# A decoder layer with product-key experts: the branch for the rest of the lists moves from the middle of the second expert product to its end

## The chip, the cores and the metric

The kernel runs on one NeuronCore of a Trainium2 chip. The metric is the device time of one launch in microseconds. Engines go by the names of the profile: PE is TensorE (PEld its weight loads), DVE is VectorE, ACT is ScalarE, POOL is GpSimd, SP is SyncE, which issues DMAs. Each engine runs its instructions in order and waits on semaphores.

## The reference

One layer for 256 tokens of width 2048: an input projection, two kinds of attention, an output projection, and then three residual steps, each with a layer norm. The change lies in the second step, the expert layer. Each token has 8 heads; each head picks 16 of 16,384 experts by two lists of 128 sub-keys.

```python
def peer_ffn(x, wq, sub_keys, u, v):
    ...
    eidx = jnp.take_along_axis(cidx, sel, axis=-1)
    gates = jax.nn.softmax(top, axis=-1)
    ...
        ub = u[eb]
        vbk = v[eb]
        act = jax.nn.gelu(jnp.einsum('thed,td->the', ub, xb).astype(jnp.float32))
        w = (gb * act).astype(xb.dtype)
        return jnp.einsum('the,thed->td', w, vbk)
...
x = layer_norm(alpha * x + ffn_out, ln_g[i, 1], ln_b[i, 1])
gate = jax.nn.sigmoid(jnp.einsum('bsd,de->bse', x, ple_gate[i]))
emb = jnp.einsum('bsk,kd->bsd', p[i], ple_proj[i])
x = layer_norm(alpha * x + gate * emb, ln_g[i, 2], ln_b[i, 2])
```

## The kernel before, in words

The expert layer treats the tokens in two ways. For 168 of them (`NDT`) all experts are computed densely; for the other 88 (`NSP`) only the chosen rows are fetched.

*Dense, u.* For each of 128 blocks of 128 experts (`u_block`, line 1130), 1 MB of `peer_u` is loaded by SyncE into one of five buffers `wf`, and 16 matmuls give the activations of 168 tokens (`ps_u`, line 212). While they run, the gates of the dense tokens are made into a table by one-hot products (`gate_work`: `ps_G`, lines 970 and 971) and multiplied onto the activations (line 987). This is done in two parts, blocks 0 to 67 and 68 to 127. Then `list_work` counts which experts any token uses and makes a list of them, for each part; the activations themselves go to memory (`s_w`).

*Dense, v.* Only listed experts are used. A block of v takes 128 of a list: GpSimd issues two gathers by index, `wc` (the activations, 86 KB) and `vf` (the rows of v, 1 MB, line 1199), and TensorE does 16 matmuls into six banks of PSUM (`ps_v`, line 1228). The plan has 46 blocks for the first list and 40 for the second (`CAPS`). A list can be longer than its plan; the overhang is counted (`total`), read into a register (line 1271), and a branch on it (`tc.If`) runs the remaining 42 blocks, or none. With these inputs it runs none. Four blocks are fetched ahead (`LEAD`), in five buffers. The last three blocks (`STAG`) are held back and done bank by bank behind the loop, so that a finished bank can be added to the residual (`v_out`), transposed (`res2`) and normed while the next one runs.

*Sparse.* The 88 tokens stand in three groups (`GROUPS`); 88 gathers of 1 MB of u rows and 88 of v rows (`gb`, line 897, four buffers) are issued by GpSimd too. VectorE multiplies and adds each (lines 865, 875), which frees the buffer. They are spread over u and v by a pace: behind every block the pace is added to `due`, and each whole number issues one gather (`gathers`). `GU` is the pace in blocks 5 to 67 of u, `GUG` in the next 38, `GUL` in the last 22, `GVG` and `GV` in v. What is left at block 32 of the second list is issued at once. The sums of groups 1 and 2 go to their place by 64 small matmuls (`third_sums`, line 929), the ones of group 0 by `natural_out`.

*Order.* Instructions wrapped in `keep` stay in the order of the program on their engine; the others are placed by a scheduler that simulates the kernel. It doesn't move instructions across the branch. On the path round the body of the branch GpSimd waits on all its eight DMA semaphores, since the body would issue DMAs on them.

*Behind the expert layer.* The gate product loads `ple_gate` into the same five buffers (`sg2.load`), splits it (lines 121 and 122) and multiplies.

Of the kernel before, what the change touches and what calls it, by code (L numbers as in the profile page):

```python
# [23 lines left out]
ND = D // P  # L24
# [32 lines left out]


GQ = 1.8
GU, GUG, GUL = 0.77, 0.80, 0.5  # L60
GV, GVG = 0.63, 0.76
GSCALE = 2.0 ** 15
GB = 3
# [4 lines left out]
STAG, LEAD, NWC = 3, 4, 8  # L68
# [92 lines left out]
def build(tc, a, out):  # L161
    nc = tc.nc
    pools = Pools(tc)
# [5 lines left out]
    def pbank(pool, name, tag="bank", bufs=4):  # L169
        return pool.tile([P, 512], F32, name=name, tag=tag, bufs=bufs)  # L170
# [653 lines left out]
    def gathers(n):  # L824

        nonlocal due
        due += n
        while due >= 1:
            due -= 1
            run(sparse, 1)  # L830
# [78 lines left out]
    def natural_parts():  # L909

        for c in range(NCH):
            parts01.append(sg2.split(ys[0], c * 512))

    def natural_out(c):

        ps = pbank(pa, "ps_yn")
        for n, part in enumerate(parts01[c]):
            keep(nc.tensor.matmul(ps[:NNAT], sel[0], part, start=n == 0, stop=n == 1))
        s = slice(c * 512, (c + 1) * 512)
        keep(nc.vector.tensor_tensor(x2[0][:NNAT, s], x2[0][:NNAT, s], ps[:NNAT], op=ALU.add))  # L920
        for j in range(2):
            keep(nc.vector.bn_stats(st2[0][:NNAT, 2 * c + j, :],
                                    x2[0][:NNAT, c * 512 + j * 256:c * 512 + (j + 1) * 256]))

    def third_sums(ps, d0, d1):

        for d in range(d0, d1):
            for i in (1, 2):
                keep(nc.tensor.matmul(ps[:, d * 32:(d + 1) * 32], ys[i][:, d * P:(d + 1) * P],
                                      sel[i], start=i == 1, stop=i == 2))  # L930

    def third_out(ps):
        n = NSP - NNAT
        dst = XF[:, :, NNAT:NSP]
        keep(nc.vector.scalar_tensor_tensor(
            dst, dst, ALPHA, ps.rearrange("p (j t) -> p j t", j=ND)[:, :, :n],
            op0=ALU.mult, op1=ALU.add))
# [184 lines left out]
    def run(work, n):  # L1122

        for _ in range(n):
            if next(work, "end") == "end":
                return True
        return False
# [51 lines left out]
    a2p = pools.open("a2p", "left", bufs=1)  # L1179
    ohp = pools.open("ohp", "left", bufs=1)  # L1180
# [10 lines left out]
    rest = [(i, b) for i, (_, n) in enumerate(PARTS) for b in range(CAPS[i], n)]  # L1191

    def v_fetch(i, b, vpool, wpool, tags):

        vf = vpool.tile([P, D], F32, name="vf", tag=tags[0], bufs=WF if vpool is sup else 2)
        wc = wpool.tile([P, NDT], F32, name="wc", tag=tags[1], bufs=NWC if vpool is sup else 2)
        for dst, src, idx in ((wc, a[f"s_w{i}"].rearrange("p a t -> (p a) t"), idxW[i]),
                              (vf, a["v_rows"], idxV[i])):
            keep(nc.gpsimd.indirect_dma_start(  # L1199
                out=dst, out_offset=None, in_=src,  # L1200
                in_offset=bass.IndirectOffsetOnAxis(ap=idx[:, b:b + 1], axis=0)))
        return vf, wc
# [24 lines left out]
    def v_mm(d, vf, wc, last):  # L1227
        return nc.tensor.matmul(psv[d // 3][:, d % 3 * NDT:(d % 3 + 1) * NDT],  # L1228
                                vf[:, d * P:(d + 1) * P], wc, start=False,
                                stop=last and (d % 3 == 2 or d == ND - 1))  # L1230
# [8 lines left out]
    def v_out(b):  # L1239

        n = min(3, ND - 3 * b)
        dst = XF[:, 3 * b:3 * b + n, NSP:]
        keep(nc.vector.scalar_tensor_tensor(
            dst, dst, ALPHA, psv[b][:, :n * NDT].rearrange("p (j t) -> p j t", j=n),
            op0=ALU.mult, op1=ALU.add))

    def v_blocks(n, wpool, between=lambda: None):

        for _ in range(n):
            while order and len(fetched) <= LEAD and (not order[0][0] or len(idxV) > 1):  # L1250
                fetched.append(v_fetch(*order.pop(0), sup, wpool, ("wf", "wc")))
            block = fetched.pop(0)
            for d in range(ND):
                v_mm(d, *block, False)
                if d % 8 == 7:
                    between()
# [10 lines left out]
    for b in range(CAPS[0]):  # L1267
        if b == CAPS[0] - LEAD:
            while not done:
                done = run(work, 1)  # L1270
            more = nc.values_load(total[0:1, 0:1], min_val=0, max_val=NIA * NKEY)
        v_blocks(1, wcp, half)
        gathers(GVG if b < 28 else GV)

    fbp = pools.open("fbp", "right", bufs=1)
    with tc.If(more > 0, preferred_fallthrough_block=False):
        for i, b in rest:
            block = v_fetch(i, b, fbp, fbp, ("vf", "wc_"))
            for d in range(ND):
                v_mm(d, *block, False)  # L1280
    pools.close("fbp", "ohp", "a2p")
    wcq = pools.open("wcq", "left", bufs=1)
    for _ in range(LEAD + 1):
        v_blocks(1, wcq)
# [11 lines left out]
    def res2(t, d0, nd):  # L1296

        ps = pbank(pp, "ps_y2")
        for j in range(nd):
            keep(nc.tensor.transpose(ps[:, j * P:(j + 1) * P], XF[:, d0 + j, t * P:(t + 1) * P],  # L1300
                                     ident))
        r = slice(0 if t else NNAT, P)
        for c in range(nd // 2):
            nc.vector.bn_stats(st2[t][r, d0 // 2 + c, :], ps[r, c * 256:(c + 1) * 256])
        nc.scalar.copy(x2[t][r, d0 * P:(d0 + nd) * P], ps[r, :nd * P])
# [11 lines left out]
    def rows2(c):  # L1317
        for i, src in enumerate(("ln_g", "ln_b")):
            keep(nc.sync.dma_start(
                gb2[c][:, i], a[src][1:2, c * 512:(c + 1) * 512].to_broadcast([P, 512])))  # L1320
# [5 lines left out]
    def res1(d0, nd):  # L1326

        ps = pbank(pa, "ps_y1")
        for j in range(nd):
            keep(nc.tensor.transpose(ps[:, j * P:(j + 1) * P], XF[:, d0 + j, :P], ident))  # L1330
        nc.scalar.mul(x2[0][:NNAT, d0 * P:(d0 + nd) * P], ps[:NNAT, :nd * P], ALPHA)
# [8 lines left out]
    N1 = CAPS[1]  # L1340
    for b in range(LEAD + 1, N1 - STAG):
        v_blocks(1, wcq)
        gathers(GV)
        if b in range(6, 14, 2):
            res1(2 * b - 12, 4)
        if b == N1 - 20:
            natural_parts()
        if b in range(N1 - 18, N1 - 14):
            natural_out(b - N1 + 18)
        if b == N1 - STAG - 5:  # L1350
            while not run(sparse, 1):
                pass
    held = list(fetched)
    assert len(held) == STAG and not order
    gw = [sg2.load(a["ple_gate"][0, i]) for i in range(2)]
    parts0 = [sg2.split(gw[0], c * 512) for c in range(4)]

    for bank in range(6):
        if bank == 1:
            ps3 = pbank(pa, "ps_y3")  # L1360
            third_sums(ps3, 0, ND)
            third_out(ps3)
        elif bank == 2:
            res2(1, 0, 2)
            res2(0, 0, 2)
        elif bank == 3:
            res2(1, 2, 4)
            res2(0, 2, 4)
            rows2(0)
            parts0 += [sg2.split(gw[1], c * 512) for c in range(4)]  # L1370
        elif bank == 4:
            res2(1, 6, 2)
            res2(0, 6, 2)
            rows2(1)
        elif bank == 5:
            res2(1, 8, 4)
            res2(0, 8, 4)
        for d in range(3 * bank, min(3 * bank + 3, ND)):
            for i, block in enumerate(held):
                keep(v_mm(d, *block, i == STAG - 1))  # L1380
        v_out(bank)
# [346 lines left out]
```

## Time and profile before

| | |
|---|---|
| three runs | 1738.1, 1739.07, 1742.0 us (median 1739.07) |
| the profiled execution | 1734.96 us, its span 1733.2 us |
| mean granted TensorE clock | 0.989 |
| busy share | TensorE 98%, VectorE 64%, GpSimd 35%, ScalarE 32% |
| DMA | 555.49 MB, mean 321 GB/s |
| u, dense product | from 559 to 1161 us of the span |
| v, dense product | from 1163 to 1623 us of the span |
| branch | at about 1400 us |

Times in the rows are microseconds from the start of the span. A block of v is 32 records of `ps_v`, two for each matmul. Idle time stands in square brackets with what ended it. A stretch shows how long each engine was busy in it, the granted clock as a share of full speed (1.00 or 0.50 at any moment) and the share of time in which the 16 DMA engines were busy.

### The profile page before, as it was taken

How to read it: one execution, taken by the hardware profiler on the slowest of the kernel's cores; microseconds unless marked ns; L12 is line 12 of the kernel's file. 1: busy time of each engine (PE TensorE's matmuls, PEld its weight loads, DVE VectorE, ACT ScalarE, POOL GpSimd, SP SyncE). 2: the span in 40 equal slices, each digit the busy share in tenths (PEclk: the TensorE clock that was granted, in tenths of full speed). 3: DMA queues.
4: the chain of work that ended last, by engine and by line, in shares of the span. 5: the costliest groups of instructions: out<-in, count | busy, mean ns of one | idle time of the engine just before them, and what ended most of it. 6: DMA issues, size and time to landing. Idle time of an engine off the chain costs nothing.

```text
span 1733.2 us, 29306 instructions
## 1 busy us (share of the span) xinstructions
PE 1696.1 (98%) x11288; PEld 1574.4 (91%) x11288; DVE 1100.7 (64%) x2299; ACT 553.9 (32%) x1392; POOL 607.2 (35%) x625
## 2 busy tenths in 40 slices
PE   9999999999999999999999999999999989997998
PEld 7888888877889999999999999999999989997786
DVE  5565588662589779744457775757777823343676
ACT  5677468743111100010035552015551001000452
POOL 0143033105235423622223232145556757683000
PEclk9999999999999999999999999999999999998999
DMA  7645644574898999999999999969999989997471
GB/s 291 197 153 167 236 150 156 168 302 140 319 419 333 410 421 418 418 421 421 420 403 387 388 378 399 421 251 405 370 375 390 416 335 407 415 345 295 154 278 49
DMA packets 97101, 555.49 MB, mean 321 GB/s; under 512 B 13360, under 2 KB 16608, under 8 KB 41504
## 3 DMA queue, kind: packets, MB, share of 16 engines
q0 software_dynamic: 43152, 285.45, 41.2%
q1 hardware_dynamic: 52080, 264.99, 40.3%
q10 hardware_dynamic: 1728, 3.15, 0.5%
q8 instruction: 91, 1.49, 0.3%
q14 instruction: 50, 0.41, 0.1%
HBM read 536.67 MB, written 17.04 MB: 319 GB/s over the span
## 4 chain that ended last, share of the span: by engine, by line
PE 80%; DMA 13%; DVE 3%; issue 2%; POOL 2%; ACT 1%; POOLq 0%; ACTq 0%; SPq 0%; DVEq 0%
PE ps_u L212 27%; PE ps_v L1228 17%; DMA wf<-peer_u 8%; PE ps_qk L200 7%; PE ps_q L212 6%; PE ps_qk L202 4%; PE ps_v L219 2%; PE ps_v L221 2%; PE ps_v L220 2%; PE ps_gate L219 1%; PE ps_gate L221 1%; PE ps_gate L220 1%; PE ps_mix L220 1%; PE ps_mix L221 1%; PE ps_mix L219 1%
## 5 line engine op out<-in xcount | busy, mean ns | idle before, releaser
L212 PE MATMUL ps_u<-XF,wf 128*128 128x168 f32 x3936 | 584.0, 308 | 6.8 <-DMA wf<-peer_u 6.0
L212 PEld LDWEIGHTS ps_u<-XF,wf 128*128 128x128 f32 x3936 | 562.6, 190 | 14.1 <-issue 8.8
L1228 PE MATMUL ps_v<-wc,vf 128*128 128x168 f32 x2752 | 420.8, 311 | 15.3 <-DMA vf<-v_rows,idxV 15.3
L1228 PEld LDWEIGHTS ps_v<-wc,vf 128*128 128x128 f32 x2752 | 399.9, 192 | 18.0 <-issue 16.8
L122 DVE TENSOR_TENSOR wl<-wf,wh 128x1024 fp32r<-128x1024 f32 (+1 forms) x199 | 212.6, 1090 | 110.4 <-ACT wh L121 109.0
L865 DVE SCALAR_TENSOR_TENSOR gb<-gb,xq 128x2048 f32<-128x2048 f32 x88 | 202.2, 2302 | 100.2 <-DMA gb<-u_rows,eig 100.1
L121 ACT CAST wh<-wf 128x1024 fp32r<-128x1024 f32 (+1 forms) x199 | 172.1, 892 | 227.5 <-DMA wf<-ple_gate 112.2
L875 DVE SCALAR_TENSOR_TENSOR y<-gb,ew,y 128x2048 f32<-128x2048 f32 x78 | 182.9, 2344 | 72.9 <-DMA gb<-v_rows,eig 72.4
L1133 ACT ACTIVATE A<-ps_u 128x168 f32<-128x168 f32 x128 | 39.5, 309 | 471.8 <-PE ps_u L212 465.7
L897 POOL DMA_INDIRECT gb<-u_rows,eig x88 | 95.1, 1081 | 261.7 <-DVE gb L865 155.7
L200 PE MATMUL ps_qk<-X,wh 128*128 128x512 f32 x512 | 185.2, 401 | 0.0
L897 POOL DMA_INDIRECT gb<-v_rows,eig x88 | 102.5, 1164 | 125.2 <-DVE eq L956 34.7
L202 PE MATMUL ps_qk<-X,wl 128*128 128x256 f32 x512 | 145.7, 285 | 0.0
L1199 POOL DMA_INDIRECT vf<-v_rows,idxV x86 | 108.3, 1259 | 87.1 <-PE ps_G L977 48.6
L962 ACT ACTIVATE hi<-eq,ghf 128x68 f16<-128x68 f16 (+1 forms) x336 | 112.8, 336 | 74.5 <-DVE eq L956 74.2
L1199 POOL DMA_INDIRECT wc<-s_w,idxW x86 | 97.3, 1131 | 56.1 <-issue 35.8
L200 PEld LDWEIGHTS ps_qk<-X,wh 128*128 128x128 f32 x512 | 96.4, 188 | 22.0 <-issue 1.0
L212 PE MATMUL ps_q<-XF,wf 128*128 128x256 f32 x512 | 115.0, 382 | 0.0
L987 DVE SCALAR_TENSOR_TENSOR A<-ps_G,A 128x18 f32<-128x18 f32 (+2 forms) x168 | 46.7, 306 | 107.4 <-PE ps_G L971 58.2
L963 ACT ACTIVATE lo<-eq,glf 128x68 f16<-128x68 f16 (+1 forms) x336 | 112.1, 334 | 0.0
L212 PEld LDWEIGHTS ps_q<-XF,wf 128*128 128x128 f32 x512 | 96.3, 191 | 13.0 <-ACT eb L581 0.7
L202 PEld LDWEIGHTS ps_qk<-X,wl 128*128 128x128 f32 x512 | 96.3, 188 | 2.5 <-issue 1.3
(316 smaller groups left out, 2137.8 us busy)
## 6 DMA issues: line engine op xcount, KB each, us to landing
wf<-peer_u SPq DMA_DIRECT2D x123, 1024.0 KB
wf<-w_qk SPq DMA_DIRECT2D x64, 512.0 KB
wf<-w_out SPq DMA_DIRECT2D x32, 512.0 KB
wf<-peer_wq SPq DMA_DIRECT2D x16, 1024.0 KB
wf<-ple_gate SPq DMA_DIRECT2D x16, 1024.0 KB
s_w<-A SPq DMA_DIRECT2D x14, 672.0 KB
wf<-w_v SPq DMA_DIRECT2D x16, 512.0 KB
wf<-w_sv SPq DMA_DIRECT2D x15, 512.0 KB
```

The costliest lines, as they stand in the source:

```text
L121: self.order(nc.scalar.copy(wh, src))
L122: self.order(nc.vector.tensor_tensor(wl, src, wh.bitcast(F32), op=ALU.subtract))
L200: nc.tensor.matmul(ps, wh[:, j * P:(j + 1) * P], xt[:, dt, :], start=dt == 0, stop=False)
L202: nc.tensor.matmul(ps[:, :T], wl[:, j * P:(j + 1) * P], xt[:, dt, :T], start=False, stop=dt == ND - 1)
L212: nc.tensor.matmul(ps[:, :T - t0], wf[:, dt * P:(dt + 1) * P], xt[:, dt, t0:], start=dt == 0, stop=dt == ND - 1)
L865: keep(nc.vector.scalar_tensor_tensor(g, g, 1.0, xq[i], op0=ALU.mult, op1=ALU.mult, accum_out=eact[i][:, j:j + 1]))
L875: keep(nc.vector.scalar_tensor_tensor(ys[i], g, ew[i][:, j:j + 1], ys[i], op0=ALU.mult, op1=ALU.add))
L897: keep(nc.gpsimd.indirect_dma_start(out=g, out_offset=None, in_=a[kind], in_offset=bass.IndirectOffsetOnAxis(ap=eig[i][:, 0, j:j + 1], axi ...
L962: nc.scalar.mul(hi[:, j, :], eq[:, j, :], ghf[:, t])
L963: nc.scalar.mul(lo[:, j, :], eq[:, j, :], glf[:, t])
L1199: keep(nc.gpsimd.indirect_dma_start(out=dst, out_offset=None, in_=src, in_offset=bass.IndirectOffsetOnAxis(ap=idx[:, b:b + 1], axis=0)))
L1228: return nc.tensor.matmul(psv[d // 3][:, d % 3 * NDT:(d % 3 + 1) * NDT], vf[:, d * P:(d + 1) * P], wc, start=False, stop=last and (d % 3 = ...
```

## The change

Four edits. The branch with its 42 blocks moves from behind the first list's blocks to behind the second loop, ahead of the three held blocks; its buffers change sides. The paces `GU` and `GUL` change from 0.77 and 0.5 to 0.75 and 0.66. What is left of the gathers is issued behind block 36 of the second list instead of 32. In the bank loop the third sums go from bank 1 to bank 2, and two `res2` trade places.

```diff
@@ -57,7 +57,7 @@
 
 
 GQ = 1.8
-GU, GUG, GUL = 0.77, 0.80, 0.5
+GU, GUG, GUL = 0.75, 0.80, 0.66
 GV, GVG = 0.63, 0.76
 GSCALE = 2.0 ** 15
 GB = 3
@@ -1271,14 +1271,7 @@
             more = nc.values_load(total[0:1, 0:1], min_val=0, max_val=NIA * NKEY)
         v_blocks(1, wcp, half)
         gathers(GVG if b < 28 else GV)
-
-    fbp = pools.open("fbp", "right", bufs=1)
-    with tc.If(more > 0, preferred_fallthrough_block=False):
-        for i, b in rest:
-            block = v_fetch(i, b, fbp, fbp, ("vf", "wc_"))
-            for d in range(ND):
-                v_mm(d, *block, False)
-    pools.close("fbp", "ohp", "a2p")
+    pools.close("ohp", "a2p")
     wcq = pools.open("wcq", "left", bufs=1)
     for _ in range(LEAD + 1):
         v_blocks(1, wcq)
@@ -1347,24 +1340,31 @@
             natural_parts()
         if b in range(N1 - 18, N1 - 14):
             natural_out(b - N1 + 18)
-        if b == N1 - STAG - 5:
+        if b == N1 - STAG - 1:
             while not run(sparse, 1):
                 pass
+
+    fbp = pools.open("fbp", "left", bufs=1)
+    with tc.If(more > 0, preferred_fallthrough_block=False):
+        for i, b in rest:
+            block = v_fetch(i, b, fbp, fbp, ("vf", "wc_"))
+            for d in range(ND):
+                v_mm(d, *block, False)
+    pools.close("fbp")
     held = list(fetched)
     assert len(held) == STAG and not order
     gw = [sg2.load(a["ple_gate"][0, i]) for i in range(2)]
     parts0 = [sg2.split(gw[0], c * 512) for c in range(4)]
 
     for bank in range(6):
-        if bank == 1:
+        if bank == 2:
+            res2(1, 0, 2)
             ps3 = pbank(pa, "ps_y3")
             third_sums(ps3, 0, ND)
             third_out(ps3)
-        elif bank == 2:
-            res2(1, 0, 2)
-            res2(0, 0, 2)
         elif bank == 3:
             res2(1, 2, 4)
+            res2(0, 0, 2)
             res2(0, 2, 4)
             rows2(0)
             parts0 += [sg2.split(gw[1], c * 512) for c in range(4)]
```

The first place is TensorE's order at the branch, with the semaphores that it waits for (`DMASW` are GpSimd's DMAs). Before, it stands behind the last block of the first list; `...` leaves out the body.

```order
L1228 MATMUL ps_v<-wc,vf 128x168 [waits DMASW4_49,DMASW3_49]
L1228 MATMUL ps_v<-wc,vf 128x168 x15
L1271 TENSOR_LOAD total [waits DVE_49]
L1276 COMPARE_AND_BRANCH
L1276 UNCONDITIONAL_BRANCH [waits PE_49]
...
L1276 UNCONDITIONAL_BRANCH
L1228 MATMUL ps_v<-wc,vf 128x168 [waits DMASW6_49,DMASW5_49]
```

In the changed kernel it stands behind the last block of the second loop, and the three held blocks follow: one matmul waits for each.

```order
L1228 MATMUL ps_v<-wc,vf 128x168 [waits DMASW7_49,DMASW6_49]
L1228 MATMUL ps_v<-wc,vf 128x168 x15
L1271 TENSOR_LOAD total [waits DVE_49]
L1348 COMPARE_AND_BRANCH
L1348 UNCONDITIONAL_BRANCH [waits PE_49]
...
L1348 UNCONDITIONAL_BRANCH
L1228 MATMUL ps_v<-wc,vf 128x168 [waits DMASW2_49,DMASW1_49]
L1228 MATMUL ps_v<-wc,vf 128x168 [waits DMASW4_49,DMASW3_49]
L1228 MATMUL ps_v<-wc,vf 128x168 [waits DMASW6_49,DMASW5_49]
L1228 MATMUL ps_v<-wc,vf 128x168 x15
L1293 MATMUL ps_y_14718<-ident,XF 128x128 [waits DVE_49]
```

The read of `total`, the compare and the jump have moved from between the lists to ahead of the held blocks. Banks 0 and 1 now run as one piece, and the third sums come behind the first transposes.

The second place is GpSimd's order at v's end: `gb` is a token gather, `wc` and `vf` are a block's two fetches. Before:

```order
L1199 DMA wc_14563<-s_w1_61,idxW1_12814 128x168
L1199 DMA vf_14562<-v_rows,idxV1_12813 128x2048
L897 DMA gb_14582<-v_rows,eig2_4050 128x2048
L897 DMA gb_14585<-v_rows,eig2_4050 128x2048
L897 DMA gb_14588<-v_rows,eig2_4050 128x2048
L1199 DMA wc_14594<-s_w1_61,idxW1_12814 128x168
L1199 DMA vf_14593<-v_rows,idxV1_12813 128x2048
L1199 DMA wc_14614<-s_w1_61,idxW1_12814 128x168
L1199 DMA vf_14613<-v_rows,idxV1_12813 128x2048
L1199 DMA wc_14634<-s_w1_61,idxW1_12814 128x168
L1199 DMA vf_14633<-v_rows,idxV1_12813 128x2048
L514 TENSOR_TENSOR ln_rstd_14879<-ln_rstd_14879,half_neg_74 128x1
```

After:

```order
L1199 DMA wc_13733<-s_w1_61,idxW1_12829 128x168
L1199 DMA vf_13732<-v_rows,idxV1_12828 128x2048
L897 DMA gb_13752<-v_rows,eig2_4050 128x2048
L1199 DMA wc_13756<-s_w1_61,idxW1_12829 128x168
L1199 DMA vf_13755<-v_rows,idxV1_12828 128x2048
L1199 DMA wc_13778<-s_w1_61,idxW1_12829 128x168
L1199 DMA vf_13777<-v_rows,idxV1_12828 128x2048
L1199 DMA wc_13798<-s_w1_61,idxW1_12829 128x168
L1199 DMA vf_13797<-v_rows,idxV1_12828 128x2048
L1348 COMPARE_AND_BRANCH
L1348 ISA
L1348 UNCONDITIONAL_BRANCH
```

Three gathers in a row stood ahead of the last three fetch pairs; now one stands there, the others are spread among the blocks ahead, and the branch follows. No gather stands behind the last fetch.

The third place is TensorE's order in u, ahead of the first gate products (`ps_gT` is a transpose of the gates, `xN` a count of matmuls); - is before, + after, and the products that follow are left out.

```order
 L807 MATMUL ps_gT<-ident,gate 128x128
-L212 MATMUL ps_u<-XF,wf 128x168 x42
+L212 MATMUL ps_u<-XF,wf 128x168 x25
 L807 MATMUL ps_gT<-ident,gate 128x128
-L212 MATMUL ps_u<-XF,wf 128x168 x288
-L970 LDWEIGHTS ohb
-L970 MATMUL ps_G<-hi,ohb 128x68
-L971 LDWEIGHTS ohb
...
+L212 MATMUL ps_u<-XF,wf 128x168 x280
+L970 LDWEIGHTS ohb
+L970 MATMUL ps_G<-hi,ohb 128x68
```

The first product stands 25 matmuls earlier than before.

## Rows read from the trace of the kernel before

**Rows 1.** The page, parts 1 and 5: TensorE's share, v's product

```profile
PE 1696.1 (98%) x11288; PEld 1574.4 (91%) x11288; DVE 1100.7 (64%) x2299; ACT 553.9 (32%) x1392; POOL 607.2 (35%) x625
...
L1228 PE MATMUL ps_v<-wc,vf 128*128 128x168 f32 x2752 | 420.8, 311 | 15.3 <-DMA vf<-v_rows,idxV 15.3
```

**Rows 2.** TensorE's waits, whole span: us in total, times, longest us

```profile
PE ps_v L1228 <- DMA vf<-v_rows,idxV: 15.3, 3, 6.6
PE ps_u L212 <- DMA wf<-peer_u: 6.0, 22, 1.1
```

**Rows 3.** Timeline, branch: start us, us, engine line ..., [idle before <-releaser]

```profile
1398.57 0.94 POOL L897 DMA_INDIRECT gb<-v_rows,eig  x1 [0.31 <-issue]
...
1406.21 9.99 PE L1228 MATMUL ps_v<-wc,vf 128*128 128x168 f32 x58 [6.61 <-DMA vf<-v_rows,idxV]
...
1408.11 1.29 DVE L873 TENSOR_SCALAR y<-gb,ew 128x2048 f32<-128x2048 f32 x1 [5.40 <-DMA gb<-v_rows,eig]
...
1410.87 0.95 POOL L1199 DMA_INDIRECT wc<-s_w,idxW  x1 [11.36 <-issue]
```

**Rows 4.** Chain that ended last, in order of time: start us, us, what

```profile
1395.31 10.31 DMA vf<-v_rows,idxV
1405.63 0.58 issue
...
1515.04 4.56 PE ps_v L1228 x32
...
1580.69 9.51 DMA vf<-v_rows,idxV
```

**Rows 5.** Stretches behind the branch: us, busy (instructions), PEclk, DMA share, GB/s

```profile
1406.00:1408.00 2.00, 1.79 (x6) 1.82 (x7) 0.00 (x0) 0.00 (x0) 0.00 (x0) 0.50 0.18 70
1408.00:1410.00 2.00, 2.00 (x11) 2.00 (x11) 1.29 (x1) 0.00 (x0) 0.00 (x0) 0.69 0.00 0
```

**Rows 6.** Timeline of GpSimd, towards v's end

```profile
1492.04 1.13 POOL L1199 DMA_INDIRECT vf<-v_rows,idxV  x1 [1.86 <-PE ps_v L1228]
...
1569.68 0.94 POOL L897 DMA_INDIRECT gb<-v_rows,eig  x1 [6.16 <-DVE gb L875]
...
1580.69 0.94 POOL L1199 DMA_INDIRECT vf<-v_rows,idxV  x1 [0.30 <-issue]
```

**Rows 7.** Timeline of TensorE, v's end and the held blocks

```profile
1529.93 50.84 PE L1228 MATMUL ps_v<-wc,vf 128*128 128x168 f32 x354
1586.10 0.90 PE L1228 MATMUL ps_v<-wc,vf 128*128 128x168 f32 x2 [5.33 <-DMA vf<-v_rows,idxV]
1590.34 3.82 PE L1228 MATMUL ps_v<-wc,vf 128*128 128x168 f32 x14 [3.34 <-DMA vf<-v_rows,idxV]
...
1604.78 5.39 PE L1228 MATMUL ps_v<-wc,vf 128*128 128x168 f32 x18
```

**Rows 8.** Stretches of u: full DMA, gate products, list work, u's end

```profile
705.00:885.00 180.00, 174.60 (x1192) 168.65 (x1191) 85.33 (x95) 18.65 (x60) 50.60 (x73) 1.00 1.01 420
885.00:1065.00 180.00, 180.00 (x1618) 177.11 (x1615) 130.63 (x263) 88.90 (x362) 57.82 (x57) 1.00 0.99 385
1065.00:1125.00 60.00, 58.95 (x433) 58.23 (x432) 39.47 (x163) 3.73 (x12) 10.01 (x15) 1.00 1.02 421
1125.00:1155.00 30.00, 30.00 (x229) 29.69 (x228) 24.00 (x75) 5.07 (x20) 8.43 (x6) 1.00 0.50 176
```

**Rows 9.** Stretches of the third sums and the bank behind them

```profile
1594.00:1597.00 3.00, 3.00 (x30) 3.00 (x28) 0.68 (x1) 0.00 (x0) 0.00 (x0) 1.00 0.00 0
1597.00:1609.00 12.00, 12.00 (x53) 12.00 (x53) 0.55 (x1) 0.00 (x0) 0.00 (x0) 0.50 0.00 0
```

**Rows 10.** The page, part 5: VectorE's use of the gate products

```profile
L987 DVE SCALAR_TENSOR_TENSOR A<-ps_G,A 128x18 f32<-128x18 f32 (+2 forms) x168 | 46.7, 306 | 107.4 <-PE ps_G L971 58.2
```

**Rows 11.** Timeline of TensorE: two neighbouring blocks of u

```profile
871.84 4.80 PE L212 MATMUL ps_u<-XF,wf 128*128 128x168 f32 x32 [1.08 <-DMA wf<-peer_u]
876.80 4.80 PE L212 MATMUL ps_u<-XF,wf 128*128 128x168 f32 x32 [0.17 <-DMA wf<-peer_u]
```

## The prediction

> **What bounds the kernel now.** I read the page first, then who waited for whom, then the timeline, the chain and short windows at each place that the diff touches. TensorE is busy 98% of the span, and one tenth of it is the expert output product `ps_v` (line 1228) [rows 1]. So whatever the change does, it can only give back the little time in which TensorE stands still or runs at the lower of its two clocks. The list of its waits shows where that is: 15.3 us in 3 waits of `ps_v` for the DMA of `vf`, and 6.0 us in 22 short waits of `ps_u` for its weights [rows 2]. The three long ones are the two places that the diff moves.
>
> The first is the branch after the first list's 46 blocks. TensorE stops at 1406.21 - 6.61 = 1399.60 and goes on at 1406.21; GpSimd issues nothing from 1399.51 to 1410.87 [rows 3]. The order says why: at the branch GpSimd waits for all eight of its DMA semaphores before it goes round the body, and TensorE's first matmul behind the branch waits for two of them. The chain agrees: it runs through a fetch issued at 1395.31 that landed at 1405.62, and 0.58 us later TensorE starts [rows 4]. That fetch is the fourth behind the block that TensorE wants next, so this is the drain and not a lack of data. Meanwhile the DMA engines run dry (share 0.18 and 0.00), and TensorE starts at half clock [rows 5].
>
> The second is v's end. TensorE finishes the last block of the loop at 1586.10 - 5.33 = 1580.77, waits 5.33 us, does one matmul, waits 3.34 us, and has all three held blocks only at 1590.34 [rows 7]. The last fetch was issued at 1580.69 and took 9.51 us [rows 4, 6]. It was late because GpSimd, which issues in order, had to issue the last three token gathers in a row before it, and the third waited 6.16 us for a free buffer [rows 6].
>
> **The change part by part.** *A, the branch leaves the middle.* TensorE's 6.61 us go, and so does the half clock behind them: 1.79 us of work at 0.50 and 2.00 us at 0.69 cost 0.90 + 0.62 = 1.5 us [rows 5]. Together 8.1 us. What is late next there would be a fetch: between the two places GpSimd was held up by TensorE not having freed a buffer (1492.04, one of five such rows from 1478 to 1510) [rows 6], so the fetches keep pace, and I take all 8.1. The other end is 0, if the DMA engines are the limit and the stall comes back later.
>
> *B, the branch comes to v's end.* Here TensorE must wait for the last `vf` anyway, so the drain itself has a cover. [...] Nobody waits behind GpSimd's drain except three loads of `em` that are wanted much later. SyncE issues the first gate load before its branch and the second behind it; it needs the buffer of the last block, which is not free earlier. VectorE's last gather products stand before its own branch. So the price is the branch c on TensorE. It is at least the 0.58 us from landing to start [rows 4] and at most the whole 6.61 us of the middle [rows 3], in which all of it was done. The nearest row is GpSimd's: VectorE's 1408.11 instruction waited for the last gather issued before the branch, and GpSimd issues again 2.76 us after that [rows 3]. TensorE has to read and compare besides, so I take c = 4. The two waits of 8.67 us become 4: gain 4.7 (bounds 2.1 and 8.1). [...]
>
> That the fetches are in time rests on the order: the three gathers in a row are gone, one gather stands before the last three fetch pairs. The last `vf` needs the buffer of the block two before the last of the loop, so it can be issued about 2 x 4.56 us (a block, [rows 4]) before TensorE gets there, plus about 1 us for its `wc`. With the 9.51 to 10.31 us of [rows 4] it lands 1.4 to 2.2 us behind TensorE's stop: inside c. The clock behind the wait falls as it does now, so nothing there.
>
> *C, the pace of the token gathers.* By the paces (each block adds its own, each whole number asks for a gather) 78 instead of 79 are asked for by block 67 of u, 113 in both by block 113, and 123 instead of 120 by block 127. From 705 to 885 the DMA engines are full and TensorE loses 180.00 - 174.60 = 5.40 us [rows 8]; a block takes 4.96 us (871.84 to 876.80) [rows 11]. A gather of 1.05 MB at 420 GB/s is 2.5 us, so one less gives up to 2.5; I take 2.0. The three more come where the DMA share falls to 0.50 [rows 8] and cost nothing; if one falls into the full stretch before 1125, it costs 2.5. Bounds -2.5 and 2.5. Three fewer gathers during v give nothing by themselves, since TensorE doesn't wait there.
>
> *D, third sums one bank later.* The same 64 small matmuls run, now behind two dense banks. In the profile the clock was full at 1594 and fell at 1597, three microseconds into them, for 12 us [rows 9]; those cost 6.0 us against full clock. I see no reason why it should not fall again: 0, with 6.0 as the other bound. The transposes of `res2` only trade places.
>
> Sum: 8.1 + 4.7 + 2.0 + 0 = 14.8 us. The profiled execution took 1734.96 us around its span of 1733.2, so it would take 1720.2. The median of the runs is 4.1 us above it: 1739.07 - 14.8 = **1724.3 us**.
>
> **The rivals.** *R1, the stall in the middle comes back.* The DMA share between the branch and v's end is near 1.0, and if that is saturation, the time given to TensorE is waited for later. A is 0, the gain 6.7, the time 1732.4. Against it stand the waits of GpSimd for TensorE. 12%.
>
> *R2, a cheap branch and a warm clock.* c is 0.6 and half of D comes too: 8.1 + 8.1 + 2.0 + 3.0 = 21.2, 1717.9. For it: the wait would be too short for the fall in clock that the 6.61 us brought. Against: the small matmuls brought one without any wait. 15%.
>
> *R3, the change doesn't do what it says.* In words the last gathers go behind v's last fetch; in the order the last one stands ahead of the last three. If it waits for a buffer as now (6.16 us, [rows 6]), the fetches are late as now, and B is 0: 10.1, 1729.0. Against it: the gathers now come one per block or two. 10%.
>
> *R4, slower: TensorE waits for the gate products in u.* The scheduler sets the first `ps_G` 25 matmuls of `ps_u` earlier. There are 56 groups of three tokens, and TensorE runs in order. If VectorE, which is held by gathers in its own order, is late for each by t, it costs 56 t; from t = 0.26 us it eats the whole gain, and at 0.35 us the time is 1739.07 - 14.8 + 19.6 = 1743.9. Against it: VectorE waits 107.4 us before its use of these products, mostly for TensorE [rows 10], and TensorE has no idle time at all from 885 to 1065 [rows 8]. 6%.
>
> **How the numbers follow.** The forecast keeps 57%, with 1720 to 1729 as its own range (c between 0.6 and 6.6, C between -2 and 2.5). R1 and R3 lie above it, R2 below, R4 far above. Leaving out R4 and the outer half of R2, the range is 1715 to 1734. Faster by more than 0.2% (3.5 us, about what can be told from no change) means below 1735.6: the forecast, R2, and nearly all of R1 and R3, 0.87. Within 0.2%: the tails of R1 and R3, 0.07. Slower: R4, 0.06.
>
> **What would show it.** Right: no idle time of TensorE and no gap of GpSimd behind the 46th block of v, the DMA share near 1 straight through; one wait of TensorE of 3 to 5 us before the held blocks instead of 5.33 and 3.34; the last `vf` issued before TensorE stops; 2 to 4 us of idle time between 705 and 885 of u. Waits for `vf` inside the second list mean R1. A last fetch that is issued after TensorE has stopped means R3. A wait of TensorE well over 6.6 us at the end would make B wrong, full clock through the third sums D, waits at `ps_G` mean R4.

## The result and the profile after

The changed kernel took 1723.7 us (median; the kernel before 1738.9 beside it): 0.9907 of the time before, 95% interval 0.9890 to 0.9924. The forecast was 1724.3. Its profiled execution took 1723.58 us around a span of 1721.8; that of before took 1734.96, which is 4.0 us under its median, so the two traces differ by 11.4 us and the medians by 15.2.

TensorE's waits after (us in total, times, longest), beside [rows 2]:

```profile
PE ps_v L1228 <- issue: 8.2, 7, 5.3
PE ps_u L212 <- DMA wf<-peer_u: 6.3, 18, 1.7
```

The 15.3 us for `vf` are gone. What stands in their place has no releaser. In the middle of v, where TensorE stood for 6.61 us and the DMA engines ran dry [rows 3, 5], the windows of after show neither (us, busy time of PE, PEld, DVE, ACT, POOL, clock, DMA share, GB/s):

```profile
1396.00:1404.00 8.00, 8.00 (x58) 8.00 (x57) 1.24 (x2) 0.00 (x0) 5.45 (x6) 1.00 1.01 414
1404.00:1412.00 8.00, 8.00 (x59) 8.00 (x58) 4.07 (x2) 0.00 (x0) 6.82 (x4) 1.00 1.01 417
```

TensorE's timeline at v's end after, beside [rows 7] (start us, us, what, idle time before):

```profile
1524.30 50.32 PE L1228 MATMUL ps_v<-wc,vf 128*128 128x168 f32 x352
1579.87 8.13 PE L1228 MATMUL ps_v<-wc,vf 128*128 128x168 f32 x36 [5.25 <-issue]
...
1597.67 5.21 PE L1228 MATMUL ps_v<-wc,vf 128*128 128x168 f32 x18
...
1611.90 1.02 PE L1228 MATMUL ps_v<-wc,vf 128*128 128x168 f32 x6
```

And GpSimd's, beside [rows 6]:

```profile
1556.68 1.37 POOL L1199 DMA_INDIRECT vf<-v_rows,idxV  x1 [1.03 <-PE ps_v L1228]
...
1565.77 0.94 POOL L1199 DMA_INDIRECT vf<-v_rows,idxV  x1 [2.37 <-PE ps_v L1228]
1575.01 1.70 POOL L1464 DMA_DIRECT2D em<-s_emb  x3 [8.30 <-PEq L1348]
```

The last fetch is issued 8.85 us before TensorE stops at 1574.62, and what holds the last fetches up is TensorE, which frees their buffers. Instead of two waits for data (5.33 and 3.34) there is one of 5.25 at the branch, and the 36 products behind it run partly at half clock, 0.66 on average:

```profile
1580.00:1588.00 8.00, 8.00 (x38) 8.00 (x39) 0.68 (x1) 0.00 (x0) 0.00 (x0) 0.66 0.59 190
```

The row of `em` dates the drain. `em` is issued when GpSimd's DMAs have landed and TensorE's sequencer has given its signal at the branch (PEq L1348), that is at 1575.01, 0.39 us after TensorE's last product. The other 4.86 us of the stop lie behind that: they are neither TensorE's wait for its own work nor GpSimd's for its DMAs.

In u the stretch that was to gain has 3.24 us of idle time instead of 5.40, and the later ones more than they had [rows 8]:

```profile
705.00:885.00 180.00, 176.76 (x1248) 171.17 (x1247) 92.71 (x117) 27.57 (x97) 53.44 (x73) 1.00 1.01 420
1065.00:1125.00 60.00, 56.85 (x418) 55.56 (x417) 47.80 (x181) 3.41 (x11) 10.48 (x16) 1.00 1.01 419
1125.00:1155.00 30.00, 29.58 (x221) 29.13 (x221) 23.11 (x62) 4.68 (x19) 13.14 (x6) 1.00 0.64 239
```

### The profile page after: what moved, and what is told of

Its sections match the earlier page's. It is cut to its first block, busy times and chain, and to the rows that moved or that the text cites. A ratio compares the mean times of both kernels' runs of the same rounds, so it can differ in the third digit from the quotient of the medians.

```text
span 1721.8 us, 29351 instructions
## 1 busy us (share of the span) xinstructions
PE 1692.1 (98%) x11288; PEld 1571.0 (91%) x11288; DVE 1102.6 (64%) x2299; ACT 553.6 (32%) x1392; POOL 630.1 (37%) x628
## 5 line engine op out<-in xcount | busy, mean ns | idle before, releaser
L897 POOL DMA_INDIRECT gb<-v_rows,eig x88 | 110.8, 1259 | 147.6 <-DVE eq L956 32.8
L1199 POOL DMA_INDIRECT wc<-s_w,idxW x86 | 113.0, 1314 | 40.2 <-issue 25.0
L212 PEld LDWEIGHTS ps_q<-XF,wf 128*128 128x128 f32 x512 | 95.9, 190 | 12.3
```

Source lines behind the costliest of these rows:

```text
L212: nc.tensor.matmul(ps[:, :T - t0], wf[:, dt * P:(dt + 1) * P], xt[:, dt, t0:], start=dt == 0, stop=dt == ND - 1)
L897: keep(nc.gpsimd.indirect_dma_start(out=g, out_offset=None, in_=a[kind], in_offset=bass.IndirectOffsetOnAxis(ap=eig[i][:, 0, j:j + 1], axi ...
L1199: keep(nc.gpsimd.indirect_dma_start(out=dst, out_offset=None, in_=src, in_offset=bass.IndirectOffsetOnAxis(ap=idx[:, b:b + 1], axis=0)))
```

## The experiments

All twelve ran against the kernel before, which took 1730.9 to 1731.7 us beside them; so ratios are compared. "Paces" are `GU` and `GUL`; the "flush" is the place where what is left of the gathers is issued at once. "v" is the time from the start of u's last `ps_u` matmul to the start of the last group of `ps_v`, from the timeline of one execution (before: 1160.6 to 1622.6; the first execution of the changed kernel: 456.0).

| kernel | us | ratio to before | interval | v, us |
|---|---|---|---|---|
| before | 1731.4 | 1 | | 462.0 |
| e1 branch moved only | 1721.5 | 0.9953 | 0.9939-0.9966 | 452.9 |
| e2 before, no branch | 1722.9 | 0.9949 | 0.9936-0.9961 | 452.9 |
| e4 paces and flush only | 1718.4 | 0.9929 | 0.9917-0.9942 | 449.6 |
| e5 third sums only | 1730.3 | 0.9995 | 0.9986-1.0004 | 461.0 |
| g3 flush only | 1730.4 | 0.9998 | 0.9986-1.0010 | 461.4 |
| f0 changed kernel again | 1717.1 | 0.9918 | 0.9901-0.9935 | 448.4 |
| f2 changed, paces as before | 1721.5 | 0.9937 | 0.9918-0.9955 | 452.2 |
| g4 changed, third sums as before | 1718.3 | 0.9919 | 0.9895-0.9944 | 449.8 |
| f1 changed, no branch | 1709.6 | 0.9873 | 0.9854-0.9893 | 440.5 |
| f3 changed, branch of one block | 1708.8 | 0.9872 | 0.9853-0.9890 | 441.3 |
| g1 changed, branch of two loops | 1710.1 | 0.9870 | 0.9849-0.9890 | 441.5 |
| g2 before, branch of two loops | 1726.8 | 0.9966 | 0.9951-0.9980 | 458.7 |

The last column follows the medians in the main: most of what the edits do happens between u's end and v's end. u itself, from the first to the last `ps_u` matmul that reads `wf`, takes 599.4 to 602.0 us in the traces with the old paces and 599.9 to 601.9 in those with the new ones, but for one (g1, 604.9, where TensorE waits 2.1 us for ScalarE).

**e1_branch**, the branch block moved from the middle to v's end as in the change, nothing else:

```
-    fbp = pools.open("fbp", "right", bufs=1)
-    with tc.If(more > 0, preferred_fallthrough_block=False):
...
-    pools.close("fbp", "ohp", "a2p")
+    pools.close("ohp", "a2p")
...
+    fbp = pools.open("fbp", "left", bufs=1)
+    with tc.If(more > 0, preferred_fallthrough_block=False):
...
+    pools.close("fbp")
     held = list(fetched)
```

> The kernel before with the branch at v's end, ahead of the three held blocks; the pace of the gathers, the place where the leftover gathers are flushed, and the third sums are as before. Theory (the middle branch is paid in full, and the branch at the end shares its wait with the late last fetch): -8.1 us in the middle, nothing at the end, where the 8.67 us of waits for the last fetches stay and hide the branch: 1738.9 - 8.1 = 1730.8. First rival (the branch alone is the whole change): 1724. Second rival (the wait in the middle comes back elsewhere in v): 1737 to 1740.

Its ratio is worth 8.1 us (1731.4 x 0.0047), as the theory said. At the end its trace has a wait of 5.55 us without a releaser and then one of 2.75 for a fetch, 8.30 in all where before had 8.67: the branch lies over most of the lateness of the fetches.

```profile
1572.30 1.46 PE L1228 MATMUL ps_v<-wc,vf 128*128 128x168 f32 x4 [5.55 <-issue]
1576.51 4.26 PE L1228 MATMUL ps_v<-wc,vf 128*128 128x168 f32 x14 [2.75 <-DMA vf<-v_rows,idxV]
```

**e2_nobr_mid**, the kernel before without its branch:

```
-    with tc.If(more > 0, preferred_fallthrough_block=False):
-        for i, b in rest: ...
```

> The kernel before without the branch (the blocks for lists that overflow are left out, which these inputs never reach). Theory (the middle branch costs 6.61 us of idle TensorE and 1.5 us at the half clock behind it, and nothing else): 1738.9 - 8.1 = 1730.8, with v's end as before. Rival (GpSimd's 11.36 us gap also delays the gathers and fetches behind it, so that more returns): 1724 to 1727. Other rival (a stall of TensorE for fetches takes its place): 1736 to 1739.

8.8 us (6.8 to 11.1): the middle branch costs what its idle time and half clock say. The waits at v's end stay:

```profile
1574.16 0.90 PE L1228 MATMUL ps_v<-wc,vf 128*128 128x168 f32 x2 [4.34 <-DMA vf<-v_rows,idxV]
1579.29 4.26 PE L1228 MATMUL ps_v<-wc,vf 128*128 128x168 f32 x14 [4.23 <-DMA vf<-v_rows,idxV]
```

**e4_gath**, paces and flush of the change, branch in the middle:

```
-GU, GUG, GUL = 0.77, 0.80, 0.5
+GU, GUG, GUL = 0.75, 0.80, 0.66
...
-        if b == N1 - STAG - 5:
+        if b == N1 - STAG - 1:
```

> The kernel before with the gathers' paces in u (.75 and .66) and the flush of the leftover gathers behind the last fetch; the branch stays in the middle, the third sums where they were. Theory (the pace is a wash, 2.2 us won and 2.1 us lost in u; the last fetches come in time, so the 5.33 and 3.34 us waits at v's end go): 1738.9 - 8.7 = 1730.2, and then this edit and the branch's (1730.8 alone) together give less than their sum, since at the end the branch takes what the fetches gave up. Rival (the last fetches are held by TensorE's buffers and not by the gathers, so the waits stay): 1737 to 1739. Other rival (the denser late gathers cost u more than they spare): 1741 or more.

More than the theory: 12.3 us. TensorE's timeline at v's end shows why; there is no wait at all for the held blocks:

```profile
1526.39 52.89 PE L1228 MATMUL ps_v<-wc,vf 128*128 128x168 f32 x370
...
1587.54 4.75 PE L1228 MATMUL ps_v<-wc,vf 128*128 128x168 f32 x18
```

The 370 products run through the held blocks, where before had waits of 5.33 and 3.34 and a clock of 0.56 behind them (1590.34 to 1594.00). The last gather is issued at 1555.82, ahead of the last three fetches. The paces without the flush were not run. Moving the branch and this pair of edits don't add: 8.1 alone and 12.3 alone give 14.2 together (f0), since what frees the fetches also takes away the branch's cover.

**e5_third**, third sums and `res2` a bank later, nothing else:

```
-        if bank == 1:
+        if bank == 2:
+            res2(1, 0, 2)
             ps3 = pbank(pa, "ps_y3")
             third_sums(ps3, 0, ND)
             third_out(ps3)
-        elif bank == 2:
-            res2(1, 0, 2)
-            res2(0, 0, 2)
         elif bank == 3:
             res2(1, 2, 4)
+            res2(0, 0, 2)
```

> The kernel before with the third sums a bank later and one pair of the transposes in bank 3, nothing else. Theory (order among TensorE's instructions that all run; the 128 small products take the clock down a bank later, which spares little while the waits at v's end have taken it down already): 1738.9, within 1.5 us. Rival (the clock stays full a bank longer): 1732 to 1736. Other rival (the sums later make their reader late at the end): 1741 or more.

0.9 us, and no change within the interval.

**g3_flush**, one line of e4:

```
-        if b == N1 - STAG - 5:
+        if b == N1 - STAG - 1:
```

> The kernel before with the flush of the leftover gathers behind the last fetch and nothing else. Theory (the flush alone frees the last fetches and takes the 8.7 us of waits at v's end; the paces are a wash): 0.994 to 0.995 of the kernel before, 1721 to 1723 where that takes 1731. Rival (with the old paces three gathers or more are left for the very end and the third sums wait for them, so that the paces are needed): 1726 to 1729.

The theory fell, and so did its account of e4. The flush alone gains nothing that can be told from no change. TensorE's timeline:

```profile
1525.33 50.89 PE L1228 MATMUL ps_v<-wc,vf 128*128 128x168 f32 x356
1579.47 3.90 PE L1228 MATMUL ps_v<-wc,vf 128*128 128x168 f32 x14 [3.25 <-DMA vf<-v_rows,idxV]
...
1586.86 0.64 PE L929 MATMUL ps_y<-sel,gb 128*128 128x32 f32 x2 [3.35 <-DVE gb L875]
```

and GpSimd's:

```profile
1562.25 2.40 POOL L1199 DMA_INDIRECT vf<-v_rows,idxV  x1 [1.91 <-PE ps_v L1228]
1564.95 0.93 POOL L897 DMA_INDIRECT gb<-v_rows,eig  x1 [0.30 <-issue]
...
1567.44 2.40 POOL L1199 DMA_INDIRECT vf<-v_rows,idxV  x1 [0.30 <-issue]
1570.14 0.94 POOL L897 DMA_INDIRECT gb<-v_rows,eig  x1 [0.30 <-issue]
```

With the old paces there are gathers left among and behind the last fetches. The last `vf` is issued at 1567.44 and TensorE goes on at 1579.47, 12.0 us later; and the last gather reaches VectorE so late that the third sums wait 3.35 us for it. One wait has become another.

**f0_after_again**, the changed kernel unchanged.

> The changed kernel as it is, once more, beside the three below. Theory (in the first traced execution TensorE had six waits of 0.3 to 1.0 us with no releaser in v's first half, and the gathers two like them; these belong to that execution and not to the code): 0.9907 of the kernel before, 1715 where that takes 1731.4, and no such waits in the new trace but the 5.25 us at the branch. Rival (they belong to where the code now lies): they are there again, 3 us or more in sum, at the same blocks.

The short waits of the first trace are not there; the branch is, at 5.47 us:

```profile
1519.71 48.76 PE L1228 MATMUL ps_v<-wc,vf 128*128 128x168 f32 x341
1573.94 7.38 PE L1228 MATMUL ps_v<-wc,vf 128*128 128x168 f32 x36 [5.47 <-issue]
```

**f2_pace_back**, the changed kernel with the paces of before:

```
-GU, GUG, GUL = 0.75, 0.80, 0.66
+GU, GUG, GUL = 0.77, 0.80, 0.5
```

> The changed kernel with the gathers' paces in u as before (.77 and .5); the flush stays behind the last fetch. Theory (the pace is a wash: what .75 wins in u's first part, .66 costs in its last; the place of the flush is what helps): 1715.3, within 1.5 us. Rival (the denser late gathers are needed, since with the old paces more are left over at v's end and the third sums wait for them): 1719 or more. Other rival (the old paces are cheaper): 1713 or less.

By the median 4.5 us are lost against f0 (the intervals overlap), 3.8 of them in v. VectorE's last gather product holds up what it has to do for bank 0, TensorE waits 1.37 us for that, and from the end of the 36 products to the next bank's it takes 13.4 us, where f0 takes 10.4. VectorE's and then TensorE's timeline:

```profile
1579.80 2.35 DVE L875 SCALAR_TENSOR_TENSOR gb<-gb,ew 128x2048 f32<-128x2048 f32 x1 [7.46 <-DMA gb<-v_rows,eig]
```

```profile
1576.48 7.36 PE L1228 MATMUL ps_v<-wc,vf 128*128 128x168 f32 x36 [6.33 <-issue]
...
1585.21 0.44 PE L1293 MATMUL ps_y<-ident,XF 128*128 128x128 f32 x2 [1.37 <-DVE XF L1243]
...
1597.28 4.64 PE L1228 MATMUL ps_v<-wc,vf 128*128 128x168 f32 x18
```

**g4_third_back**, the changed kernel with e5's edit undone (`if bank == 2:` is `if bank == 1:` again, `res2` as before).

> The changed kernel with the third sums and one pair of transposes a bank earlier, as before. Theory (order only, worth nothing in the kernel before: 0.9995, 0.9986 to 1.0004): 0.9907 to 0.992 of the kernel before, 1715 to 1717 where that takes 1731. Rival (now that TensorE no longer waits for fetches there, the last gathers land too late for sums a bank earlier, or the clock falls earlier): 1719 or more.

No difference from f0 (0.9919 and 0.9918).

**f1_nobr_end**, the changed kernel without the branch (e2's edit, at v's end).

> The changed kernel without the branch (the blocks for lists that overflow are left out, which these inputs never reach). Theory (the 5.25 us that TensorE idles at the branch is all on the path, and the clock behind it stays full a little longer): 1715.3 - 5.3 - 0 to 2 = 1708 to 1710. Rival (the last fetched block lands 1.4 to 2.2 us after TensorE has stopped, so that a wait of that length takes the place of the branch's): 1712. Other rival (the branch's wait only stood for a fetch that lands at that time): 1715.

The theory's number. The price of the branch at v's end is 1717.05 - 1709.59 = 7.5 us: 5.47 us of wait, and 36 products in 7.38 us that take 5.37 at full clock (f3 below). In its trace TensorE passes the place without a stop, so the last fetch had landed by then:

```profile
1519.76 53.89 PE L1228 MATMUL ps_v<-wc,vf 128*128 128x168 f32 x377
```

**f3_short_body**, one line ahead of the branch:

```
+    rest = rest[:1]
     fbp = pools.open("fbp", "left", bufs=1)
```

> The changed kernel with one block instead of 42 inside the branch (41 blocks for lists that overflow are left out, which these inputs never reach), so that what is jumped over is 1/42 as long. Theory (the price of the branch is the drain of the engines' work and the jump itself, and doesn't hang on the length of what is skipped): TensorE idles about 5.2 us there, 1715. [...]

The theory fell: 1708.8 us is as fast as with no branch (f1, 1709.6). The engines still read `total`, compare, and TensorE still waits for its own work and for the same three fetches; 16 matmuls instead of 672 are jumped over:

```profile
1567.04 5.37 PE L1228 MATMUL ps_v<-wc,vf 128*128 128x168 f32 x36 [0.54 <-PEq L1349]
```

GpSimd has fewer DMAs to wait for too, since it waits for those whose semaphores the body would use, and this body would issue two DMAs. That does not explain the gain: `em` comes 0.39 us behind TensorE's last product here and 0.39 in f0, but from there TensorE needs 5.08 us in f0 and 0.15 here. GpSimd in f0, then in f3:

```profile
1568.86 1.70 POOL L1464 DMA_DIRECT2D em<-s_emb  x3 [8.30 <-PEq L1348]
```

```profile
1566.89 1.70 POOL L1465 DMA_DIRECT2D em<-s_emb  x3 [8.31 <-PEq L1349]
```

**g1_loop**, all 42 blocks kept, as two loops whose body is one block; the list is shifted by one column in each turn:

```
-        for i, b in rest:
-            block = v_fetch(i, b, fbp, fbp, ("vf", "wc_"))
+        for i, (_, n) in enumerate(PARTS):
+            c = CAPS[i]
+            with tc.For_i(c, n, 1):
+                block = v_fetch(i, c, fbp, fbp, ("vf", "wc_"))
...
+                for idx in (idxV[i], idxW[i]):
+                    nx = fbp.tile([P, n - c - 1], U32, name="nx", tag="nx", bufs=2)
+                    nc.vector.tensor_copy(nx, idx[:, c + 1:n])
+                    nc.vector.tensor_copy(idx[:, c:n - 1], nx)
```

> The changed kernel with the 42 blocks inside the branch written as two loops of one block each, so that the same work stands there in 32 matmuls instead of 672. Theory (the price of the branch is that of the long body that is jumped over; with one block TensorE idled 0.5 us): 0.987 to 0.989 of the kernel before, 1708 to 1712 where that takes 1731, and the wait at the branch 2 us or less. Rival (the loops bring barriers and counters of their own, which are paid though the branch isn't taken): 1715 or more, as with the long body.

0.9870, with an interval below that of f0: the version that beats both. Its wait at the branch:

```profile
1573.48 5.37 PE L1228 MATMUL ps_v<-wc,vf 128*128 128x168 f32 x36 [0.68 <-PEq L1348]
```

These inputs never enter the branch, so neither the loops' speed nor what they compute is shown.

**g2_loop_mid**, the kernel before with the same loops in its branch in the middle.

> The kernel before, branch in the middle, paces, flush and third sums as before, with the 42 blocks inside the branch written as two loops of one block each. Theory (what the branch in the middle cost was the length of its body, not its place): 0.995 of the kernel before as with no branch at all, 1722 to 1724 where that takes 1731. Rival (the place costs too, since every engine drains there and the fetches behind it are late): 1727 or more.

At the branch the theory holds for TensorE. TensorE, then GpSimd, then VectorE:

```profile
1397.02 3.23 PE L1228 MATMUL ps_v<-wc,vf 128*128 128x168 f32 x21 [0.68 <-DMA wc<-s_w,idxW]
```

```profile
1394.93 0.94 POOL L897 DMA_INDIRECT gb<-v_rows,eig  x1 [0.30 <-issue]
1399.66 0.95 POOL L1199 DMA_INDIRECT wc<-s_w,idxW  x1 [3.79 <-issue]
```

```profile
1405.15 1.48 DVE L873 TENSOR_SCALAR y<-gb,ew 128x2048 f32<-128x2048 f32 x1 [6.08 <-DMA gb<-v_rows,eig]
```

TensorE waits 0.68 us instead of 6.61, and GpSimd's gap is 3.79 us instead of 11.36. But GpSimd's drain is not the same here: it goes on at 1399.66, while the gather that it issued at 1394.93 lands only when VectorE's wait ends at 1405.15. In the kernel before it went on 2.76 us behind the landing of its last gather [rows 3]. The two loops would issue four DMAs, so GpSimd waits for fewer. How much of its gap was the drain and how much the length of the body isn't separated. The time the kernel takes is worse than expected: 1726.8, close to the rival. The trace has the rest at v's end: waits of 6.51 and 3.32 us for the last fetches (e2: 4.34 and 4.23), and the third sums at half clock throughout (0.50 from 1584 to 1598), 13.5 us from their start to the next bank's products (e2: 10.4, with 0.66 from 1583 to 1594). Its runs spread from 1720.9 to 1729.8, so how much of that is the code's stays open.

## Why the prediction came out right, and where it was wrong

The sum was right: 14.8 us forecast, 15.2 measured, 14.2 in f0. Its terms were not, and that they add up is in part luck. Without the move of the branch the forecast's terms give 10.7 (8.67 and 2.0), where e4 measured 12.3; for the move they give 4.1 (8.1 less the 4 of c), where e4 and f0 differ by 1.9. One error nearly cancels the other.

*A, the middle, 8.1 us: right in size (e2: 8.8, e1: 8.1), wrong in cause.* I read the 6.61 us as the drain: GpSimd waits for all its DMAs, and TensorE for two. GpSimd's drain there is real, but TensorE does not wait for it: it goes on at 1406.21, GpSimd at 1410.87 [rows 3], and in e1, at v's end, TensorE at 1572.30 and GpSimd at 1578.98. With a short body in the same place TensorE waits 0.68 us (g2), though GpSimd's drain is shorter there too; at v's end, where GpSimd goes on at the same moment with either body, the stop is 5.47 us over the long one and 0.54 over the short one (f0, f3). So what cost TensorE the time is the length of the body that is skipped.

*B, v's end.* Three statements. That c is the one wait left: right, 5.25 and 5.47 us instead of the 4 taken, inside the bounds; the 4 was an estimate, and the reading and comparing that it adds don't make it up (f3, which does both, has 0.54). That the last `vf` lands 1.4 to 2.2 us behind TensorE's stop: wrong, f1 shows no wait, and in the first trace GpSimd, which waits for it, goes on 0.39 us after the stop. And that the fetches are in time because the three gathers in a row are gone: this is the step that failed. g3 takes those three apart by the same line and gains 0.3 us, nothing that can be told from no change. What frees the fetches needs the paces as well, which I put under C.

*C, the paces.* I put 2.0 us into u and wrote that "three fewer gathers during v give nothing by themselves, since TensorE doesn't wait there". The first half failed, and the second as far as the runs go. u gains 2.2 us from 705 to 885, and loses 2.1 from 1065 to 1125 and 0.4 from 1125 to 1155: my lower bound, a gather that falls into the full stretch. And fewer gathers in v count: paces and flush together are worth 12.3 us (e4), the flush 0.3 (g3), so with the flush in place the paces are worth 12.0; by themselves they were not run. TensorE doesn't wait for the gathers themselves before v's end, but GpSimd issues its last fetches among the ones left over. Against a v without any wait at its end, the branch moved to the end costs 7.5 us in full, which eats nearly all that the middle gives. Between e4 and f0 the move is worth 1.9 us, within the error of both.

*D, 0: right* (e5 and g4 show no change within their intervals).

*The rivals.* R1: no trace of the changed kernel has waits for `vf` in the second list. R3: the fetches are held by TensorE's buffers and issued before it stops. R4: TensorE's only waits at `ps_G` are three short ones, 1.9 us in all, without a releaser, and f0 has none. R2 did not happen (c is 5.3, not 0.6), but f3 and g1 show it as possible with a short body: 0.54 and 0.68 us, the 36 products in 5.37 us in both (in g1 at a clock of 1.00, from 1560 to 1580), and 1709 to 1710.

One thing stays open. Beside the branch the first trace of the changed kernel has nine short waits without a releaser from 1168 to 1308, 4.8 us in sum (six of `ps_v`, three of `ps_G`), and its v takes 456.0 us where f0 takes 448.4. None of the twelve later traces has them, so the code alone doesn't make them. That execution took as long as the other three timed beside it (1721.7 to 1724.2), so they need not be its alone; what causes them isn't known.

## What to carry to other kernels

Before a wait at a branch is read as a drain, make the skipped body short and look again: the same branch, at the same place in TensorE's order, cost TensorE 5.5 us over 672 matmuls and 0.5 to 0.7 over 16 or 32, and a loop gives that with the rare path still in the program. Look also at which engine's drain it is, and whether the engine that stands still waits for it. Two edits that each remove a wait at the same place have to be priced together (8.1 and 12.3 us alone, 14.2 together): the first takes away what the second would have been hidden under. And a background stream that nobody waits for still sets when the last foreground transfer lands (with the flush in place the paces are worth 12.0 us, e4 against g3), so count what is left of it at the stage's end.

## What the runs showed of the hardware

A branch whose body is skipped stops TensorE for 5.25 to 6.33 us at v's end when the body is long (after 5.25, g4 5.4, f0 5.47, e1 5.55, f2 6.33), and for 6.61 in the middle (before); over a short body it stops it for 0.54 to 0.68 (f3, g1, g2). The runs show that the length decides, by 4.9 us between f0 and f3, not what the engine does in that time.

The traces show TensorE's granted clock at two levels, 1.00 and 0.50 [rows 9]; a value between is the mean of a stretch. Around and behind the wait of 5.47 us in f0 it was 0.66 on average from 1570 to 1580 and 0.99 from 1580 to 1585, and the 36 products took 7.38 us. Behind the wait of 0.68 us in g1 it was 1.00 from 1560 to 1580, and they took 5.37; behind the wait of 0.54 us in f3 they took 5.37 too. So the long wait cost 2.0 us more than its length.
